# adaLN vectors turned by TensorE ahead of use, and two new written orders, in a hybrid encoder block

## The chip, the core and the metric

The kernel runs on one NeuronCore of a Trainium2 chip. The metric is the device time of one execution in microseconds (us). Five engines work side by side, each on its own list of instructions: TensorE (PE in the profile; its weight loads are PEld), VectorE (DVE), ScalarE (ACT), GpSimd (POOL, hardly used here) and SyncE (SP), whose list holds all DMA issues of this kernel.

## What is computed

One layer for 256 tokens of width 2048, in float32:

```
mod = silu(c) @ w_ada + b_ada                  # nine vectors of 2048: sh1 sc1 gt1 sh2 sc2 gt2 sh3 sc3 gt3
f = swiglu(modulate(rms_norm(h, g_ffn1), sh1, sc1), w1_gate, w1_up, w1_down)
h = h + 0.5 * gt1 * f
qkv = modulate(rms_norm(h, g_mix), sh2, sc2) @ w_qkv
o = concat(rms_norm(neighbourhood heads 0-7), rms_norm(dilated heads 8-15))
h = h + gt2 * (o @ w_o)
f = swiglu(modulate(rms_norm(h, g_ffn2), sh3, sc3), w2_gate, w2_up, w2_down)
h = h + 0.5 * gt3 * f
```

swiglu(x) = (silu(x @ w_gate) * (x @ w_up)) @ w_down with a hidden width of 5632; modulate(n, shift, scale) = n * (1 + scale) + shift.

## The kernel before, in words

**Products.** Every large product is made of three in a faster 32-bit format: an operand is split into a rounded high part (ScalarE, a cast) and the rest (VectorE, a subtraction), and high x high, high x low and low x high are summed. Weights come in chunks of 128 x 1024 (512 KB): `wraw` loads one into one of five "raw" buffers, `wsplit` casts it (`hiw`, L162) and subtracts (`low`, L165), which frees the raw buffer. The class `W` hands them out in order: `prepare(ahead)` splits chunks up to `ahead` (3) beyond the one in use, `chunk` returns the next. Split chunks have four buffers each.

**Stages.** (1) The first FFN's up-projection on hidden blocks 0 to 31, its down-projection, the up-projection on blocks 32 to 43 and their down-projection (`ffn_rest`, `ffn_down`). A down-projection goes through four pieces q = 0 to 3 of 512 output columns; piece by piece the residual `hq` is updated (`update`, L238 and L241), squared for the next norm (L254) and multiplied by the scale (`scaled`, L258). (2) q, k and v of four head groups, 96 units of one chunk each (`qkv_unit`), with the heads' attention (`head`: a transposes q and k, b makes scores and softmax, c transposes the weights, d multiplies v) spread over later units by the tables PLAN; then 32 units of `w_o` (`wo_unit`). LAST is unit 111, END unit 127. (3) The second FFN, as (1).

**The two boundaries.** From FFN to q, k, v, and from `w_o` to the second FFN, `cross` writes out the order of TensorE, VectorE and ScalarE by hand. The last four chunks of the old product (A) are done for the first half of the tokens, then for the second, so that norms of the first half can begin early. `Edge` does the norm: `most` and `rstd` the statistics, `normed(q, t)` the modulated norm of column quarter q for token half t (L281), `turned` four transposes on TensorE (L286), `split` the high and low parts of the result (L188, L189). Four chunks B of the next product follow for half 0 and then half 1 (`bpass`). `prep1` splits one chunk (cast and subtraction side by side in each engine's order), `extra` splits two of them into spare tiles, `keep_warm` issues matmuls on ones. Two of four quarters of half 1 are turned between the passes.

**The adaLN vectors.** `mod` is made of 144 dots on VectorE (L145), each over a 1 MB piece of `w_ada` loaded by SP (`ada_issue`, L135); vector j is complete after its 16 dots, as a tile `mods[j]` of 128 partitions x 16 columns. They run in the background: `bg_add` queues them, `bg_step` and `bg_use` issue a load or do a dot, at a rate per prepared chunk (`ws.pace`: RA, RB, RBD, RF) or at the units in COLUMNS; `bg_until(0)` does all that is queued. Vectors 0 and 1 go first, then 2, 4, 3, 5 and ten dots of 7 and 6, then the other 22 of 7 and 6 in the attention, and 8 in the second FFN. `begin`, which starts a boundary, sets the rate to zero, so dots left over then run in the attention, the last of them by `bg_until(0)` at unit LAST - 16.

Vectors 2 to 8 are needed as rows, the same 2048 numbers on every partition. `line_of(j)` writes the tile to DRAM as 16 x 128 numbers by one DMA whose access pattern swaps the two axes (L117), and `rows_of` reads the line back onto all partitions (L123).

**Who orders what.** Outside the written stretches a scheduler orders each engine's list from the program's order and a cost estimate. In the attention only TensorE's list is in program order (MANUAL); around both boundaries TensorE's, VectorE's and ScalarE's are (BORDER); SP's list is always the scheduler's. PSUM has eight banks, used as four pairs ("pair") in the up-projections and as eight single banks ("bank") elsewhere; `psum_pool` changes over.

Of the kernel before, what the change touches and what calls it, by code (L numbers as in the profile page):

```python
# [9 lines left out]
F32 = mybir.dt.float32  # L10
# [21 lines left out]
Q = 4  # L32
# [13 lines left out]
RF = 0.14  # L46
# [12 lines left out]
def build(tc, a):  # L59
    nc = tc.nc  # L60
    with ExitStack() as ctx:
# [105 lines left out]

        def wsplit_halves(raw, alloc):

            his, los = [], []  # L170
            for i in range(2):
                his.append(alloc("hih"))
                los.append(alloc("loh"))
                r = raw[:, i * QW : (i + 1) * QW]
                nc.scalar.copy(his[i], r)
                nc.vector.tensor_tensor(los[i], r, his[i].bitcast(F32), ALU.subtract)
            return his, los
# [65 lines left out]
        class Edge:  # L243
# [16 lines left out]
            def most(self, t):  # L260

                a, b = self.c[:, t, 0:1], self.c[:, t, 1:2]
                nc.vector.tensor_tensor(a, self.ss[:, t, 0:1], self.ss[:, t, 1:2], ALU.add)
                nc.vector.tensor_tensor(a, a, self.ss[:, t, 2:3], ALU.add)
# [23 lines left out]
            def split(self, q, t):  # L288
                b = self.bank[q, t].rearrange("p (k s) -> p k s", k=4)
                ts = slice(t * P, (t + 1) * P)  # L290
                split(b, nq[q][:, :, 0, ts], nq[q][:, :, 1, ts])

        def tok(ps, two, w, first, last, ts=(0, 1)):
# [19 lines left out]
            for t, l, r, st, sp_ in todo:  # L313
                nc.tensor.matmul(ps[t], l, r, start=st, stop=sp_)  # L314

        def cross(ps, twos, first, upd, edge, bpass, extra, after=None):
# [5 lines left out]
            edge.most(0)  # L322
            edge.most(1)
            ws.extra(2, extra)

            def rest(t):
                upd(t)
                edge.square(Q - 1, t, ps[t])
                edge.rstd(t)
# [4 lines left out]
            rest(0)  # L334
            edge.normed(0, 0)
            edge.normed(1, 0)
# [12 lines left out]
            ws.prep1()  # L349
# [842 lines left out]
```

## Time and profile before

| | us |
|---|---|
| median of 3 runs (lowest to highest) | 1957.53 (1956.42 to 1958.87) |
| the profiled execution | 1957.54 |
| its span, from the first to the last instruction | 1955.8 |
| PE busy | 1904.0 (97%) |
| DVE busy | 1483.8 (76%) |
| ACT busy | 889.0 (45%) |
| 16 DMA engines busy, queue q1 | 73.1% of their span |

A row of the waits tells who waited for whom, the sum in us, how often, and the longest. A row of the windows begins with the stretch in us from the span's start and its length, then for PE, PEld, DVE, ACT and POOL the busy time and number of instructions, then the granted TensorE clock (1.00 is full), the DMA engines' busy share and GB/s; a window of one line's instructions has that engine alone. A row of the timeline has start, length, engine, line, operation, out<-in, shape, number, and in brackets the idle time before it with what ended it. A row of the groups has the number of instructions, busy us, mean ns of one, and idle time before them. A DMA row has the number, KB each, and the median us from issue to landing. A row of the chain of waits has start, length and what it was.

### The profile page before, as it was taken

To read this page: it belongs to the slowest core of one execution; us is meant where nothing else is said; L and a number is where in the kernel's file an instruction comes from. 1 tells how busy PE (TensorE), PEld (TensorE's weight loads), DVE (VectorE), ACT (ScalarE), POOL (GpSimd) and SP (SyncE) were. 2 spreads that over 40 slices of the span, in tenths; PEclk is the share of its full clock that TensorE was granted. 3 is DMA by queue.
4 is the path that set the end of the run, shared out by engine and by line. 5 is a ranking of instruction groups with operands and counts; after the bars stand their busy time and mean duration, and the time that the engine had idled before them with its cause. 6 is when DMAs were issued, how large, how long until landed. Compare 5 with 4: busy or idle time off the path is not lost.

```text
span 1955.8 us, 25965 instructions
## 1 busy us (share of the span) xinstructions
PE 1904.0 (97%) x9868; PEld 1629.5 (83%) x9868; DVE 1483.8 (76%) x1940; ACT 889.0 (45%) x1293; POOL 0.7 (0%) x6
## 2 busy tenths in 40 slices
PE   9999999999999989899999798999999999999999
PEld 8888888888888878788878687788888888888887
DVE  6999999898788857888887886667676754555664
ACT  2544544434344434455555454545445443334542
POOL 0000000000000000000000000000000000000000
PEclk9999999999999999999999899999999999999999
DMA  9998888999889886688776773567767666555553
GB/s 399 403 355 321 324 310 314 300 367 401 308 345 345 316 213 207 224 332 296 249 254 208 211 260 128 170 234 244 237 244 246 229 201 209 194 186 191 193 196 139
DMA packets 138124, 513.38 MB, mean 262 GB/s; under 512 B 28176, under 2 KB 28688, under 8 KB 119568
## 3 DMA queue, kind: packets, MB, share of 16 engines
q1 hardware_dynamic: 138000, 511.74, 73.1%
q8 instruction: 77, 1.26, 0.3%
q14 instruction: 47, 0.39, 0.1%
HBM read 509.53 MB, written 2.15 MB: 262 GB/s over the span
## 4 chain that ended last, share of the span: by engine, by line
PE 66%; DVE 3%; DMA 2%; ACT 1%; issue 1%; SPq 0%; ACTq 0%
PE pb L543 20%; PE pd L314 17%; PE pb L537 10%; PE pqk L314 4%; PE pqv L314 4%; PE pqq L314 4%; PE po L314 3%; DMA rw<-in_w_e_dram 1%; DMA rw<-in_w_o_dram 1%; DVE low L165 1%; PE po L185 1%; PE pt L286 0%; ACT hiw L162 0%; SPq L135 0%; PE psc L185 0%
## 5 line engine op out<-in xcount | busy, mean ns | idle before, releaser
L165 DVE TENSOR_TENSOR low<-rw,hiw 128x1024 fp32r<-128x1024 f32 x640 | 774.3, 1221 | 334.1 <-ACT hiw L162 310.8
L162 ACT CAST hiw<-rw 128x1024 fp32r<-128x1024 f32 x640 | 669.6, 1052 | 671.5 <-PE pd L314 181.7
L543 PE MATMUL pb<-nq,hiw 128*128 128x512 f32 x2032 | 495.4, 390 | 1.1 <-DVE gu L588 0.7
L543 PEld LDWEIGHTS pb<-nq,hiw 128*128 128x128 f32 x2032 | 374.3, 188 | 74.3 <-DVE gu L588 1.0
L314 PE MATMUL pd<-hiw,hd 128*128 128x512 f32 x1408 | 352.7, 391 | 6.6 <-ACT hiw L162 5.7
L314 PEld LDWEIGHTS pd<-hiw,hd 128*128 128x128 f32 x1408 | 265.9, 189 | 62.8 <-ACT hiw L162 6.1
L537 PEld LDWEIGHTS pb<-nq,low 128*128 128x128 f32 x2032 | 262.1, 192 | 13.8 <-DVE low L165 5.3
L537 PE MATMUL pb<-nq,low 128*128 128x256 f32 x2032 | 269.9, 283 | 3.7 <-DVE low L165 3.7
L145 DVE CUSTOM_DVE_ANT_0 ra<-ra,cb,vec 128x2048 f32<-128x2048 f32 x111 | 260.2, 2344 | 7.5 <-DMA ra<-in_w_ada_dram 7.5
L314 PE MATMUL pd<-low,hd 128*128 128x512 f32 x704 | 190.7, 391 | 2.0 <-DVE low L165 2.0
L314 PEld LDWEIGHTS pd<-low,hd 128*128 128x128 f32 x704 | 132.5, 189 | 30.8 <-DVE low L165 3.2
L543 PE MATMUL pb<-nq3b,hiw 128*128 128x512 f32 x336 | 90.0, 390 | 0.0
L145 DVE CUSTOM_DVE_ANT_0 rx<-rx,cb,vec 128x2048 f32<-128x2048 f32 x33 | 77.4, 2345 | 3.0 <-DMA rx<-in_w_ada_dram 2.9
L543 PEld LDWEIGHTS pb<-nq3b,hiw 128*128 128x128 f32 x336 | 63.1, 188 | 13.6
L543 PE MATMUL pa<-nq,hiw 128*128 128x512 f32 x288 | 72.3, 393 | 0.0
L314 PE MATMUL po<-hiw,ox 128*128 128x512 f32 x256 | 68.5, 405 | 1.0 <-ACT hiw L162 1.0
L314 PE MATMUL pqk<-hiw,nq 128*128 128x512 f32 x256 | 65.0, 396 | 0.0
L314 PE MATMUL pqq<-hiw,nq 128*128 128x512 f32 x256 | 64.6, 394 | 0.0
L314 PE MATMUL pqv<-hiw,nq 128*128 128x512 f32 x240 | 62.0, 397 | 0.0
L543 PEld LDWEIGHTS pa<-nq,hiw 128*128 128x128 f32 x288 | 51.9, 189 | 9.3
L314 PEld LDWEIGHTS po<-hiw,ox 128*128 128x128 f32 x256 | 48.1, 193 | 12.0 <-ACT hiw L162 1.4
L587 ACT COPY gu<-pb 128x512 f32<-128x512 f32 x54 | 31.8, 588 | 54.7 <-PE pb L543 30.1
(192 smaller groups left out, 1592.0 us busy)
## 6 DMA issues: line engine op xcount, KB each, us to landing
ra<-in_w_ada_dram SPq DMA_DIRECT2D x111, 1024.0 KB, 7.0
rw<-in_w_b_dram SPq DMA_DIRECT2D x200, 512.0 KB, 4.6
rw<-in_w_d_dram SPq DMA_DIRECT2D x128, 512.0 KB, 5.2
rw<-in_w_c_dram SPq DMA_DIRECT2D x96, 512.0 KB, 4.3
rw<-in_w_qkv_dram SPq DMA_DIRECT2D x96, 512.0 KB, 4.9
rx<-in_w_ada_dram SPq DMA_DIRECT2D x33, 1024.0 KB, 7.5
rw<-in_w_e_dram SPq DMA_DIRECT2D x48, 512.0 KB, 4.6
rw<-in_w_a_dram SPq DMA_DIRECT2D x44, 512.0 KB, 6.2
```

Source lines behind the costliest of these rows:

```text
L145: dot = nc.vector.tensor_tensor_reduce(out=raw, in0=raw, in1=cb, scale=1.0, scalar=vec[:, BA + i : BA + i + 1], op0=ALU.mult, op1=ALU.add, ...
L162: cast = nc.scalar.copy(hi, raw)
L165: nc.vector.tensor_tensor(lo, raw, hi.bitcast(F32), ALU.subtract)
L185: nc.tensor.matmul(out, l, r, start=first and i == 0, stop=last and i == 2, **kw)
L314: nc.tensor.matmul(ps[t], l, r, start=st, stop=sp_)
L537: nc.tensor.matmul(out[:, :S], weights(b, 1), r[:, 0, :], start=False, stop=stop, skip_group_check=self.shared)
L543: nc.tensor.matmul(out, weights(b, 0), r, start=first, stop=last and b in early, skip_group_check=self.shared)
L587: nc.scalar.copy(u, p[..., :S])
```

## The change

- `line_of` transposes `mods[j]` on TensorE into a PSUM tile of 16 x 128, copies it to SBUF on VectorE (into a buffer with the tag "nt"), and writes it to DRAM in runs of 128 numbers.
- Lines 4 and 3 are made right after the first down-projection (before: in `begin`, after the second up-projection), line 5 at unit 66 (before 88), lines 7 and 6 at unit LAST - 8 (before LAST - 4), line 8 three hidden blocks before the end of the second FFN's first up-projection (before: after it). RF goes from 0.14 to 0.16.
- In the first FFN's second down-projection, `bg_until(0)` stands at piece q = 1.
- `prep1` and `extra` become `cast` and `sub`, placed apart from each other in `cross`; `split` of an edge becomes `hi` and `lo`. `cross` has a new order; half 1 of quarter 0 is turned inside the last pass of half 0; both halves of quarter 3 are turned in `end`; `keep_warm` is gone.
- Units 4 and 5 after the first boundary prepare one chunk ahead; so do chunks k = 8 to 11 after the second, which are handled one at a time (`group` 1, before 2).
- At the second boundary quarter 2 is scaled in `normed`; the last of the A chunks is prepared ahead of the updates; `bpass2` does the low weights of chunks 2 and 3 once for all 256 tokens instead of twice for 128.
- Heads 0 to 7 are scaled into float32 tiles that lie in the places of heads 12 to 15, and split into high and low at units 78, 80, ... 92.

```diff
-RF = 0.14
+RF = 0.16
...
         def line_of(j):
             lines[j] = dram.tile([KT, P], F32, tag=f"line{j}", name=f"line{j}")
-            nc.sync.dma_start(lines[j].rearrange("k p -> p k"), mods[j])
+            ps = pools["p"].tile([KT, P], F32, tag="b", name="lt")
+            nc.tensor.transpose(ps, mods[j], ident)
+            t = sp.tile([KT, P], F32, tag="nt", name="lt")
+            nc.vector.tensor_copy(t, ps)
+            nc.sync.dma_start(lines[j], t)
...
-            for t, l, r, st, sp_ in todo:
+            for i, (t, l, r, st, sp_) in enumerate(todo):
+                if i == 4 and mid:
+                    mid()
                 nc.tensor.matmul(ps[t], l, r, start=st, stop=sp_)
...
+            e = edge
...
+            ws.cast(extra)
+            ws.cast(extra)
+            ws.sub()
+            e.most()
+            upd(0)
+            e.square(Q - 1, 0, ps[0])
+            ws.sub()
+            e.rstd(0)
+            e.normed(0, 0)
+            e.normed(1, 0)
+            second(0)
+            ws.cast()
+            ws.sub()
             second(1)
             second(2)
-            edge.turned(0, 0)
+            e.turned(0, 0)
             second(3)
-            edge.turned(1, 0)
-            edge.split(0, 0)
-            edge.split(1, 0)
-            rest(1)
+            e.turned(1, 0)
+            e.hi(0, 0)
+            ws.cast()
+            e.lo(0, 0)
+            upd(1)
             if after:
                 after()
-            ws.prep1()
-            edge.normed(0, 1)
+            e.hi(1, 0)
+            e.square(Q - 1, 1, ps[1])
+            ws.sub()
+            e.lo(1, 0)
+            e.rstd(1)
+            e.normed(0, 1)
+            e.normed(1, 1)
+            ws.cast()
             B = [ws.take() for j in range(4)]
-            for j in range(3):
-                bpass(j, B[j], 0)
-            edge.turned(0, 1)
-            edge.split(0, 1)
-            bpass(3, B[3], 0)
-            keep_warm(2)
-            edge.normed(1, 1)
+            for j in range(4):
+                bpass(j, B[j], 0, (lambda: e.turned(0, 1)) if j == 3 else None)
+            e.hi(0, 1)
+            e.lo(0, 1)
+            e.normed(2, 0)
             bpass(0, B[0], 1)
...
+            e.turned(1, 1)
+            e.hi(1, 1)
+            ws.cast()
+            e.lo(1, 1)
+            e.normed(2, 1)
+            ws.sub()
             bpass(1, B[1], 1)
...
+            e.turned(2, 0)
+            e.turned(2, 1)
             bpass(2, B[2], 1)
...
             bpass(3, B[3], 1)
...
+            e.hi(2, 0)
+            e.hi(2, 1)
+            e.lo(2, 0)
+            e.lo(2, 1)
+            e.normed(3, 0)
+            e.normed(3, 1)
+            ws.sub()
 
             def end():
-                edge.turned(3, 1)
-                edge.split(3, 1)
+                for t in range(2):
+                    e.turned(3, t)
+                for t in range(2):
+                    e.hi(3, t)
+                    e.lo(3, t)
...
+                if edge is not None and q == 1:
+                    bg_until(0)
...
             ffn_down(range(F1), hid, row)
+            if begin:
+                line_of(4)
+                line_of(3)
...
-            units[u](ws.chunk())
+            units[u](ws.chunk(1 if u < 6 else None))
...
-                            edge[0].scaled(q, t)
+                            if q < 2:
+                                edge[0].scaled(q, t)
...
+                if b == 0:
+                    for hd in range(8):
+                        at(78 + 2 * hd, lambda hd=hd: split(raw_o[hd], ox[hd][:, 0, :], ox[hd][:, 1, :]))
...
+                    if hd < 8:
+                        nc.scalar.activation(raw_o[hd], po, AF.Copy, scale=go)
...
-                    if u == 88:
+                    if u == 66:
                         line_of(5)
...
-                    if u == LAST - 4:
+                    if u == LAST - 8:
                         line_of(7)
                         line_of(6)
+                    if u == END - ST:
+                        ws.prepare()
...
                 for half in range(2):
+                    if half and mid:
+                        mid()
+                    if half and j > 1:
+                        if t == 0:
+                            return
+                        ts = slice(0, S)
...
+            ws.group, ws.turn = 1, False
             for k in range(8, KT):
                 for f in range(NG):
                     for j in range(2):
+                        ws.ahead = 1 if k < 12 else AHEAD
                         ws.add(ps2[f][j], nx[k], False, k == KT - 1, key=(f, j))
...
         for f in range(NG, F1):
+            if f == F1 - 3:
+                ws.pace(0.0)
+                bg_until(0)
+                line_of(8)
             ps = pair("pb")
...
-        ws.pace(0.0)
-        bg_until(0)
-        line_of(8)
         ffn_rest(hid, 8, out=a["out"])
```

More of the change, by code (lines that the diff above doesn't have):

```diff
@@ L166, in wsplit @@
             return hi, lo
[L168 to L177, printed above, removed]
         def part_of(w, c, n):
@@ L286, in turned, with halves, hi, lo @@
                     nc.tensor.transpose(self.bank[q, t][:, j * P : (j + 1) * P], self.n[q, t][:, j * P : (j + 1) * P], ident)
-            def split(self, q, t):
+            def halves(self, q, t):
                 b = self.bank[q, t].rearrange("p (k s) -> p k s", k=4)
-                ts = slice(t * P, (t + 1) * P)
-                split(b, nq[q][:, :, 0, ts], nq[q][:, :, 1, ts])
-        def tok(ps, two, w, first, last, ts=(0, 1)):
+                return (b, *(nq[q][:, :, i, t * P : (t + 1) * P] for i in range(2)))
+            def hi(self, q, t):
+                b, hi, lo = self.halves(q, t)
+                nc.scalar.copy(hi, b)
+            def lo(self, q, t):
+                b, hi, lo = self.halves(q, t)
+                nc.vector.tensor_tensor(lo, b, hi.bitcast(F32), ALU.subtract)
+        def tok(ps, two, w, first, last, ts=(0, 1), mid=None):
             def whi(i):
@@ L358, in cross @@
-            edge.normed(1, 1)
-            bpass(0, B[0], 1)
-            edge.turned(1, 1)
-            edge.split(1, 1)
-            edge.normed(2, 0)
-            ws.prep1()
+            e.hi(1, 0)
[6 more added lines that the diff above has]
+            ws.cast()
+            B = [ws.take() for j in range(4)]
+            for j in range(4):
+                bpass(j, B[j], 0, (lambda: e.turned(0, 1)) if j == 3 else None)
@@ L466, in __init__ @@
                 self.thens = []
+                self.casts = []
                 self.ready = {}
@@ L474, in __init__, with cast, sub @@
                 self.ended_lo = False
-            def extra(self, n, alloc):
-                for i in range(n):
-                    assert self.head == self.tail + i
-                    self.ready[self.head] = wsplit_halves(wraw(srcs[self.head]), alloc)
-                    self.head += 1
-            def prep1(self):
-                self.ready[self.head] = wsplit(wraw(srcs[self.head]))
+            def cast(self, alloc=None):
+                raw = wraw(srcs[self.head])
+                if alloc:
+                    tiles = [(alloc("hih"), alloc("loh"), raw[:, i * QW : (i + 1) * QW]) for i in range(2)]
+                    self.ready[self.head] = [t[0] for t in tiles], [t[1] for t in tiles]
+                else:
+                    hi = wp.tile([P, CW], F32R, tag="whi", bufs=LOB, name="hiw")
+                    lo = wp.tile([P, CW], F32R, tag="wlo", bufs=LOB, name="low")
+                    tiles = [(hi, lo, raw)]
+                    self.ready[self.head] = hi, lo
+                for hi, lo, r in tiles:
+                    nc.scalar.copy(hi, r)
+                self.casts.append(tiles)
                 self.head += 1
+            def sub(self):
+                for hi, lo, r in self.casts.pop(0):
+                    nc.vector.tensor_tensor(lo, r, hi.bitcast(F32), ALU.subtract)
             def take(self):
@@ L791, in build @@
                     units.append(qkv_unit(len(units), g, j, nm, cch, st_))
-        end = ffn_rest(hid, 2, begin, order=order, bpass=lambda j, w, t: units[j](w, (t,)),
+        end = ffn_rest(hid, 2, begin, order=order, bpass=lambda j, w, t, mid=None: units[j](w, (t,), mid),
                        extra=lambda nm: hp.tile([P, QW], F32R, tag="hid", name=nm))
         for u in range(4, 8):
-            units[u](ws.chunk())
+            units[u](ws.chunk(1 if u < 6 else None))
             if u == 4:
@@ L816, in na_bias @@
                 return t
[L818 removed]
+            ox = [ac.tile([P, 2, S], F32R, tag=f"ox{i}", name=f"ox{i}") for i in range(12)]
+            raw_o = [ac.tile([P, 2, S], F32, tag=f"ox{i}", name=f"ro{i}") for i in range(12, NH)]
+            raw_o = [raw_o[i // 2][:, i % 2, :] for i in range(8)]
             ost = [Stat(), Stat()]
```

48 lines of the change are left out of this document (13 added, 35 removed).

## The prediction

> **What bounds the kernel now.** I read the core's span, then who ended TensorE's waits, then busy time in windows around each long wait. The span is 1955.8 us; the profiled execution took 1957.54 us, 1.74 us more, and that is also the median of the runs shown (1957.53 us). So the sum below is made against 1957.54.
>
> ```profile
> core 0: 1955.8 us, clock 0.992
> ```
> ```profile
> PE pT L896 <- DVE qn L854: 13.6, 3, 8.2
> PE pt L286 <- DVE gs L281: 13.0, 8, 2.9
> PE pd L314 <- ACT hiw L162: 5.7, 1, 5.7
> PE pb L537 <- DVE low L165: 3.7, 3, 2.1
> PE pP L937 <- DVE sc L931: 3.0, 2, 1.7
> ```
>
> The columns are: who waited, for whom, us in total, times, longest. TensorE sets the time, and there is little besides its own work to win: these five causes hold 39.0 us of waiting, 2% of the span. The question is therefore how much of 39 us the edit removes, and what it puts there. The same waits by place (us of the window, then PE busy; the clock stands after the five engines):
>
> ```profile
> 350.00:412.00 62.00, 59.15 (x301) 49.88 (x301) 55.96 (x78) 25.03 (x34) 0.00 (x0) 0.97 0.90 297
> 700.00:720.00 20.00, 14.31 (x62) 11.68 (x61) 4.73 (x6) 3.57 (x5) 0.00 (x0) 0.85 0.80 155
> 769.00:808.00 39.00, 33.71 (x157) 26.66 (x157) 27.77 (x48) 15.52 (x26) 0.00 (x0) 0.96 0.41 144
> 915.00:1030.00 115.00, 109.06 (x528) 90.50 (x527) 96.49 (x184) 60.76 (x135) 0.00 (x0) 1.00 0.72 254
> 1095.00:1121.00 26.00, 15.32 (x62) 11.88 (x61) 19.06 (x38) 6.03 (x7) 0.00 (x0) 0.80 0.80 231
> 1186.00:1243.40 57.40, 47.32 (x291) 40.81 (x289) 38.07 (x60) 23.11 (x39) 0.00 (x0) 0.97 0.38 128
> ```
>
> Window less PE busy gives idle: 2.85, 5.69, 5.29, 5.94, 10.68 and 10.08 us. After five of the waits the granted clock is 0.50 for a while:
>
> ```profile
> 389.90:393.20 3.30, 3.30 (x13) 2.91 (x13) 3.30 (x5) 2.01 (x3) 0.00 (x0) 0.50 0.87 323
> 714.20:720.90 6.70, 5.26 (x12) 4.13 (x13) 3.93 (x6) 3.45 (x6) 0.00 (x0) 0.50 1.02 403
> 785.90:789.20 3.30, 2.90 (x9) 2.51 (x10) 1.47 (x3) 0.59 (x1) 0.00 (x0) 0.50 0.43 159
> 1106.70:1116.80 10.10, 4.05 (x10) 3.08 (x11) 8.80 (x21) 2.68 (x3) 0.00 (x0) 0.50 0.74 160
> 1229.60:1232.90 3.30, 3.30 (x11) 2.62 (x10) 1.92 (x2) 1.53 (x2) 0.00 (x0) 0.50 0.02 6
> ```
>
> Work at half clock takes twice as long, so half of PE busy is lost there: 1.65, 2.63, 1.45, 2.03, 1.65 us. Idle and half clock together, by place: **350** 4.50, **700** 8.32, **769** 6.74, **915** 5.94, **1095** 12.71, **1186** 11.73. These are the prizes.
>
> **The written lines (350, 700, part of 1095).** Each adaLN vector goes to DRAM as one DMA that swaps partitions and columns, so every element is its own run:
>
> ```profile
> ra<-in_w_ada_dram SPq DMA_DIRECT2D x111, 1024.0 KB, 7.0
> ...
> out_dram<-hq SPq DMA_DIRECT2D x2, 128.0 KB, 1.9
> ...
> line<-m SPq DMA_DIRECT2D x7, 8.0 KB, 15.6
> ```
>
> 8 KB take 15.6 us, while 128 KB written in long rows take 1.9. Lines 4 and 3 are issued at the end of the first layer's second up-projection, and behind them a weight load hangs in the chain of waits:
>
> ```profile
> 695.58 18.87 DMA rw<-in_w_e_dram
> ...
> 1885.75 65.29 PE pd L314 x288
> ```
>
> The second row gives the price of a 512-wide matmul: 65.29 / 288 = 0.227 us, so a twelve-matmul down or qkv chunk is 2.72 us. With runs of 512 B the line write should land like the 1.9 us row, and it is written a whole up-projection earlier. I take all 8.3 at 700 (at worst 5.0, if the row loads, which stay, delay these chunks instead), and 3.0 of 4.5 at 350 (0 to 4.5): there line 2 is still written next to the down-projection's first loads, and VectorE is busy 55.96 of 62 us, a second reason for that wait.
>
> **The dots moved.** `bg_until(0)` now stands in the second down-projection, pieces 1 on. The code queues 32 + 64 + 10 = 106 dots ahead of the attention's own 22. By the rows below (x counts each dot and its accumulator read) 98 are done by 700 us, so eight move there, five with their loads, as three buffers can be full before. Six ran at 1075 until now:
>
> ```profile
> 0.00:700.00 700.00, 230.46 (x196) 1.00 0.89 340
> ...
> 1075.00:1112.00 37.00, 14.12 (x12) 0.93 0.80 268
> ```
> ```profile
> L165 DVE TENSOR_TENSOR low<-rw,hiw 128x1024 fp32r<-128x1024 f32 x640 | 774.3, 1221 | 334.1 <-ACT hiw L162 310.8 <-issue 15.1 <-PE pg L537 3.3
> ...
> L145 DVE CUSTOM_DVE_ANT_0 ra<-ra,cb,vec 128x2048 f32<-128x2048 f32 x111 | 260.2, 2344 | 7.5 <-DMA ra<-in_w_ada_dram 7.5
> ```
>
> Each dot holds VectorE 2.34 us. In 1095 to 1121 TensorE waits for the last group's normed q (`qn`, 13.6 us with one earlier wait), which sits in VectorE's queue behind such dots, and they wait for loads that share the DMA engines with lines 7 and 6. With no dot and no slow line there, a wait like those of 915's window should be left: three share 5.94 us, each behind one dot; I leave 1.5. Gain 11.2 (8 to 12.7). At the new place the eight dots need 8 x 2.34 = 18.7 us of VectorE. Room:
>
> ```profile
> 725.00:769.00 44.00, 44.00 (x196) 36.44 (x195) 32.72 (x39) 22.88 (x33) 0.00 (x0) 1.00 0.74 239
> ```
>
> 11.3 us idle there and, once the weight wait is gone, 15.3 in 700:720, some of it filled by the lows that the wait held back. It just fits, with three chunks of prepared weights as slack; cost 1.0 (0 to 7, all the overflow of 18.7 over 11.3).
>
> **First boundary (769).** Second half's norm waits behind a weight split:
>
> ```profile
> 784.36 1.23 DVE L165 TENSOR_TENSOR low<-rw,hiw 128x1024 fp32r<-128x1024 f32 x1 [0.52 <-ACT hiw L162]
> 785.50 0.74 DVE L281 SCALAR_TENSOR_TENSOR gs<-gs,e1c,row 128x512 f32<-128x512 f32 x1
> ```
> ```profile
> 786.30 1.11 PE L286 MATMUL pt<-ident,gs 128*128 128x128 f32 x4 [2.79 <-DVE gs L281]
> ...
> 803.53 0.70 PE L314 MATMUL pqv<-hiw,nq 128*128 128x512 f32 x2
> ```
>
> I put the new VectorE order on this clock, with 1.22 us for a weight's low, 0.74 for a norm and somewhat less for the other 128x512 operations. Until the turn of (1,0) nothing changes, since the norms of half 0 still wait for the update and its square. From there:
>
> VectorE now does the third weight's low, the lows of (0,0) and (1,0), the update of half 1, then waits for ScalarE's square of it, does the fourth weight's low (1.23 us, with 0.52 idle ahead) and only then the norm of (0,1). In the new order the update comes before the low of (1,0), 1.3 us earlier, and this low and the fourth weight's fill the time of the square. So the norm of (0,1) starts at 785.50 - 1.23 - 0.52, with the earlier update about 783.4, and ends at 784.1. TensorE asks for it four matmuls (0.9 us) later than now, at 784.2: no wait in place of 2.79. Then 0.3 us are lost until half 1 of quarter 0 is copied out. The norm of (2,0) runs in VectorE's idle time before the (1,1) low; that of (2,1) ends at 789.3, 0.4 us after TensorE has reached its turn. Both norms of quarter 3 are ready at 794.8, ahead of unit 4's end at 795.3, and both its turns follow. Unit 5, at 803.53 now, would start at 796.1, 7.4 us earlier (0.5 of it the dropped warm-up matmuls). The shorter lead of weights at units 4 and 5 costs nothing as long as a low stays under a chunk's 2.72; loads go out as raw buffers come free, not with the cast. The schedule leaves no room for hand-overs between engines, so I take 6.0 (2.9 to 7.4).
>
> **Second boundary (1186).** The same order, with three more edits: the last chunk is prepared ahead of the updates; the third quarter's scaling leaves VectorE's queue there; and two pairs of narrow groups become one wide group each:
>
> ```profile
> 1205.62 1.20 PE L1042 MATMUL pg<-nq,hih 128*128 128x256 f32 x8
> 1206.65 1.00 PE L1042 MATMUL pg<-nq,loh 128*128 128x128 f32 x8
> ```
>
> Of the narrow groups four at 1.00 become two at 1.20: 1.6 us. By the same hand schedule 0.5 us of waiting is left at the first turn, 1.4 where (0,1) must be copied out with no other matmul to put in front, 0.6 at (2,1), 0.8 before the next stage's first product as now, and 0.4 elsewhere: 3.7. The chunks of k = 8 to 11 no longer stand behind the last turn. From 11.7 + 1.6 - 3.7, and some pipeline fill at each wait saved, I get 10.5 (4.8 to 13.3, the upper end with no wait left).
>
> **The cost of turning.** Seven transposes join TensorE's work, seven copies VectorE's. Eight narrow matmuls in a row take 1.00 us (0.13 each), four transposes after a wait 1.11 (0.28 each): 0.9 to 2.0 us. I take 1.0, by the row without a wait, for the vectors are complete by then. Dearer may be the PSUM buffer. Lines 2, 4 and 3 stand right where the pools change, so the next stage's first accumulator may have to wait for VectorE's copy, queued behind updates. Four operations of 128x512, 0.74 us each as in row 785.50, at two places make 5.9 us; if the scheduler gives another buffer, it is nothing. I take 1.5, nearer to nothing: the stages change over without such a wait in the five causes above. Lines 5 (unit 66) and 7, 6 (unit 103) have fixed places in TensorE's order, long after their last dots; SP issues three small writes there, landing like the 1.9 us row under the units that follow, and line 5's rows are loaded 29 units later as now. Line 8 is turned three column blocks before its stage ends instead of in the next: counted as nothing. Each copy holds one of two "nt" buffers until its write has landed; the tanh that shares them comes once in four chunks, 10.9 us.
>
> **Heads split later (915).** Eight splits leave VectorE's queue in the stretch with the waits for `sc` (3.0 us in two) and come back at units 78 to 92, two units apart; each is 128x256, so half of the 0.74 us of twice the size. ScalarE, 60.76 of 115 us busy, gets eight more casts. The parked outputs take the places of heads 12 to 15, needed 16 units after the last split: no wait. VectorE's order there is the scheduler's, and the dots stay in the columns: gain 1.0 (-3 to 3).
>
> **Sum.** 3.0 + 8.3 + 11.2 + 6.0 + 10.5 + 1.0 = 40.0 gained; 1.0 + 1.5 + 1.0 = 3.5 paid; 36.5 net: 1957.54 - 36.5 = **1921 us**.
>
> **Half clock.** Rows 389.9 and 785.9 show it after waits of no more than 2.1 and 2.8 us, so by these rows one or two of the waits that I leave may cost 1.6 us each on top, and the time would be 1924. [...]
>
> **Rivals.** (1) The boundaries' waits move rather than go: VectorE's chain, 27.77 of 39 us busy, stays what ends last. For it: every wait there names VectorE. Against: the written order puts weight lows behind norms. Then they give 2.9 and 4.8, 8.8 us less: 1930. (2) Loads, not lines, starve the stages: five ada loads beside the w_e chunks, and row loads which still follow their line on SP. Then 8.3, 3.0 and half of 11.2 stay lost, 16.9: 1938. Against: 8 KB at 15.6 us. (3) Slower: the scheduler queues the moved loads and dots in series. Place: second down-projection, piece 1. A load takes 7.0 us and its dot 2.34; five in series and three more dots make 53.7 us, less a lead of three chunks (8.2): 45.5 us of wait, and 1957.5 - 36.5 + 45.5 = 1966. It decides once four of the five loads run so; up to then the gains pay for it. For: lows wait behind dots in VectorE's queue. Against: dots at 1075 to 1112 ran six in 37 us. (4) The lines stay in step with the old waits because turns are scheduled as late as the DMAs were, and the boundary gains are eaten by new bank waits: about 1957.
>
> **How the numbers follow.** Chances: forecast 0.58, (1) 0.20, (2) 0.12, (3) 0.06, (4) 0.04. A change of 0.2%, 3.9 us, is about what a measurement can tell. Faster is forecast, (1) and (2): 0.90; same 0.04; slower 0.06. The lower end takes the upper bounds of all gains (4.5 + 8.3 + 12.7 + 7.4 + 13.3 + 3 = 49.2) at no cost: 1908. The upper end reaches past (2) to 1940. (3), (4) and the tails of (2) are left out, under 2 in 10.
>
> **What would show it.** Line writes landing in 2 to 4 us; no wait of TensorE over 2 us near 710, 1100 or 1230; no dots between 806 and 812 or after unit 85; first wide chunk after the second boundary some 35 us earlier. Wrong would be: half clock near the second down-projection, pd or pb waiting for the copy of a turned line, or a boundary as long as now.

## The result, and the profile after

The changed kernel takes 1925.80 us (median of 6 runs, 1922.57 to 1927.67); the kernel before, run beside it, 1956.98 (1955.99 to 1960.31). The ratio is 0.9835, with a 95% interval of 0.9822 to 0.9847: 31 us faster. The forecast was 1921 in 1908 to 1940. The profiled executions are 35.0 us apart (1957.54 and 1922.57), where 36.5 was forecast; what follows compares these two. The profiled execution of the changed kernel is the fastest of its six, so the medians are only 31.2 us apart.

Span and clock of the changed kernel, and TensorE's longest waits by cause (waiting tile, releaser, us in total, times, longest):

```profile
core 0: 1920.8 us, clock 0.997
```
```profile
PE pd L316 <- DVE lt L120: 7.2, 1, 7.2
PE pt L279 <- DVE gs L274: 2.7, 3, 1.8
PE pd L316 <- DVE low L169: 2.7, 2, 1.6
PE pd L316 <- ACT hiw L166: 2.3, 2, 1.9
PE pT L927 <- DVE qn L881: 2.2, 1, 2.2
```

The two causes that led the list before, `qn` with 13.6 us and `gs` with 13.0, are down to 2.2 and 2.7. On top stands a wait that was not there: `lt` is the turned line in PSUM. The same places by window (us of the window, PE busy, weight loads, VectorE, ScalarE, GpSimd, granted clock, DMA share, GB/s):

```profile
350.00:412.00 62.00, 54.83 (x285) 47.16 (x284) 58.58 (x82) 25.20 (x34) 0.00 (x0) 0.92 0.84 301
390.20:400.40 10.20, 5.01 (x12) 3.97 (x13) 10.20 (x16) 2.27 (x4) 0.00 (x0) 0.50 0.83 286
700.00:745.00 45.00, 41.13 (x194) 33.64 (x193) 38.28 (x44) 19.54 (x25) 0.00 (x0) 1.00 0.88 336
769.00:808.00 39.00, 38.40 (x183) 31.19 (x183) 31.44 (x50) 19.76 (x33) 0.00 (x0) 1.00 0.57 192
905.00:1020.00 115.00, 112.66 (x549) 93.75 (x548) 98.61 (x188) 64.65 (x146) 0.00 (x0) 1.00 0.75 261
1075.00:1101.00 26.00, 26.00 (x123) 21.28 (x123) 19.74 (x42) 13.78 (x34) 0.00 (x0) 1.00 0.65 215
1170.00:1227.40 57.40, 53.59 (x346) 47.88 (x346) 44.55 (x69) 30.72 (x50) 0.00 (x0) 1.00 0.44 153
```

Around 1095 TensorE is busy in every one of 26 us (15.32 of 26 before), in the first boundary 38.40 of 39 (33.71). Only the first row is worse than its twin: idle went from 2.85 to 7.17 us, and one stretch at half clock is left, of 10.2 us, where there were five. The written lines land in 2.7 us by the median, as forecast, but single ones took 1.4 to 8.7 us (lines 4 and 3 the longest):

```profile
line<-lt SPq DMA_DIRECT2D x7, 8.0 KB, 2.7
```

To compare stretches that have moved, I call the **excess** of a stretch the sum, over its matmuls, of the time from one start to the next less the median of that time for matmuls of the same line and shape. It holds idle time and half clock alike.

| stretch of the work | excess before | after | gained | on record |
|---|---|---|---|---|
| 350 to 412, first down-projection begins | 5.9 | 9.9 | -4.1 | 3.0, less part of 1.5 |
| 412 to 700 | 3.1 | 3.2 | -0.1 | 0 |
| 700 to 745, second down-projection begins | 8.5 | 4.8 | 3.7 | 8.3 less 1.0 |
| 745 to 812, first boundary | 7.9 | 1.4 | 6.5 | 6.0 |
| 812 to 1030, attention | 7.8 | 4.1 | 3.6 | 1.0 |
| 1030 to 1121 | 14.0 | 1.7 | 12.3 | 11.2 |
| 1121 to 1250 (1240 after), second boundary | 15.8 | 6.1 | 9.7 | 8.9 |
| second layer's down-projection begins | 1.3 | 0.0 | 1.3 | 0 |
| fewer and wider matmuls, less the turns | | | 2.3 | 1.6, less 1.0 |

The terms add up to 35.2; the rest, -0.2, lies spread over the other stretches. A second execution of the same program (e5 below) has an excess of 8.8, 6.1 and 5.8 us in the first, third and fifth row, so these rows are good to some 1.7 us; the last section shows why.

### The profile page after: what moved, and what is told of

The parts are those of the page before. It is cut to its first block, busy times and chain, and to the rows that moved or that the text cites. A ratio compares the mean times of both kernels' runs of the same rounds, so it can differ in the third digit from the quotient of the medians.

```text
span 1920.8 us, 25930 instructions
## 1 busy us (share of the span) xinstructions
PE 1893.1 (99%) x9851; PEld 1623.1 (84%) x9851; DVE 1484.4 (77%) x1939; ACT 891.5 (46%) x1301; POOL 0.7 (0%) x6
## 4 chain that ended last, share of the span: by engine, by line
PE 69%; DVE 2%; DMA 1%; ACT 0%; issue 0%; SPq 0%; ACTq 0%; DVEq 0%
PE pb L565 20%; PE pd L316 16%; PE pb L559 11%; PE pqk L316 5%; PE pqq L316 5%; PE pqv L316 4%; PE po L316 4%; PE pg L1086 1%; PE psc L178 1%; PE po L178 1%; DMA ra<-in_w_ada_dram 0%; DMA row<-line 0%; PE pg L565 0%; PE pP L968 0%; PE pt L279 0%; PE pT L927 0%
## 5 line engine op out<-in xcount | busy, mean ns | idle before, releaser
L169 DVE TENSOR_TENSOR low<-rw,hiw 128x1024 fp32r<-128x1024 f32 x632 | 764.7, 1221 | 307.4 <-ACT hiw L166 291.8
L166 ACT CAST hiw<-rw 128x1024 fp32r<-128x1024 f32 x632 | 661.3, 1052 | 652.0 <-PE pd L316 205.6
L149 DVE CUSTOM_DVE_ANT_0 ra<-ra,cb,vec 128x2048 f32<-128x2048 f32 x109 | 255.6, 2345 | 6.9 <-DMA ra<-in_w_ada_dram 6.8
L149 DVE CUSTOM_DVE_ANT_0 rx<-rx,cb,vec 128x2048 f32<-128x2048 f32 x35 | 82.1, 2345 | 3.3 <-DMA rx<-in_w_ada_dram 3.3
L565 PEld LDWEIGHTS pb<-nq3b,hiw 128*128 128x128 f32 x336 | 63.1, 188 | 13.6
```

What stands on the lines that cost most here:

```text
L149: dot = nc.vector.tensor_tensor_reduce(out=raw, in0=raw, in1=cb, scale=1.0, scalar=vec[:, BA + i : BA + i + 1], op0=ALU.mult, op1=ALU.add, ...
L166: cast = nc.scalar.copy(hi, raw)
L169: nc.vector.tensor_tensor(lo, raw, hi.bitcast(F32), ALU.subtract)
L565: nc.tensor.matmul(out, weights(b, 0), r, start=first, stop=last and b in early, skip_group_check=self.shared)
```

## The experiments

Eleven kernels ran, each in several rounds beside the kernel before, whose median was 1957.7, 1958.6 and 1958.1 us in the three sets. Ratios are to it. The program of the changed kernel was measured twice, as itself and as e5: 0.9835 and 0.9824, 2 us apart, and smaller differences of medians are not read. In the texts on record, A and B are the two explanations that a run was to tell apart.

### Line 2's turn: which PSUM buffer it takes

The new wait, in the timeline of the changed kernel (start, us, engine, line, operation):

```profile
387.95 0.27 PE L118 MATMUL lt<-ident,m 128*16 128x128 f32 x1
388.95 0.42 DVE L614 SCALAR_TENSOR_TENSOR pt<-th,pt 128x256 f32<-128x256 f32 x1
389.29 2.35 DVE L149 CUSTOM_DVE_ANT_0 ra<-ra,cb,vec 128x2048 f32<-128x2048 f32 x1
...
393.50 1.22 DVE L169 TENSOR_TENSOR low<-rw,hiw 128x1024 fp32r<-128x1024 f32 x1
394.63 0.42 DVE L614 SCALAR_TENSOR_TENSOR pt<-th,pt 128x256 f32<-128x256 f32 x1
394.97 0.27 DVE L120 COPY lt<-lt 16x128 f32<-16x128 f32 x1
395.39 3.75 PE L316 MATMUL pd<-hiw,hd 128*128 128x512 f32 x8 [7.17 <-DVE lt L120]
```

In the kernel before the line's DMA left at 354, soon after the last of its dots; a turn has a place in TensorE's order, and that is 388. Its copy stands in VectorE's queue behind a dot, a weight's low and the folds of two column blocks, 6 us of work without a gap, and `pd` waits for the copy. Does it wait because of the turn, or because VectorE is full?

**e1_line2_early**: 1923.38 us, ratio 0.9827 (0.9815 to 0.984).

```diff
             for f in range(NF1, F1):
+                if f == F1 - 4:
+                    line_of(2)
                 ps = pair("pb")
...
         hid = ffn(K1, part, rest1)
-        line_of(2)
```

> Edit: the changed kernel with line 2's turn moved from behind the first layer's first up-projection to four column blocks before its end (its last dot is done at 337.7 us, the turn stands at 387.9 in the changed kernel). Theory A, the turned line's PSUM buffer: the 7.2 us wait of the first down-projection product is the wait for a 0.27 us copy that stands behind a queue of VectorE work, and the half clock behind it follows from it. Then both go: the excess over the matmuls' own pitch between 350 and 412 us, 9.9 us in the changed kernel, falls to 1 to 3 us, no half clock stands there, and the time is 7 to 9 us under the changed kernel's median of 1925.8: 1917 to 1919. Rival B, VectorE is simply full there: the first products wait for the weights' lows or the hidden state in the place of the copy, the excess stays at 6 or more, and the time is 1922 to 1926.

The wait for the copy went, and another took its place (waits by cause):

```profile
PE pd L319 <- DVE pt L608: 5.8, 1, 5.8
```

Excess 8.9: B by its numbers. But the releaser is telling: it is the fold of the very last accumulator of the up-projection (the fold adds an accumulator to the hidden tile on VectorE, and frees its bank). The built programs, not the traces, list the bank of every PSUM tile. The pairs come in the order 0, 6, 4, 2 (first bank of each), and the first `pd` of the new pool always takes bank 0:

```
                  last accumulators, in order      first pd (bank 0) follows
before            0, 6, 4, 2                       the fourth-last accumulator
changed kernel    0, 6, 4, 2, line 2 in 0          the line
e1                line 2 in 0; 6, 4, 2, 0          the last accumulator
e9 (below)        0, 6, 4, 2, warm in 0, line in 6 the warm-up matmul, which nobody reads
```

So the line's place in the pool's rotation decides, not its place in time. **e5_skip_pair** (1924.53 us, 0.9824, 0.9811 to 0.9838) was meant to test that:

```diff
+        pair("skip")
         line_of(2)
```

> Edit: one line in the changed kernel: a PSUM pair is allocated and not used just before line 2 is turned, so that the turned line takes the second of the four pairs in place of the first. Theory A, the turn shifts the rotation: 56 accumulators went through four pairs before, so the first down-projection product, which always takes the first banks of the new pool, followed the fourth-last accumulator; with the line as 57th it follows the line itself, and with the line moved ahead it followed the very last accumulator (5.8 us). With the skipped pair it follows the fourth-last again: the wait of pd for the line's copy goes, the half clock shrinks to one step or none, the excess between 350 and 412 us goes from 9.9 to 2 to 4, and the time is 1917 to 1921. Rival B, VectorE's backlog: ten operations stand in its queue whichever bank is used, so pd waits for a low or a fold there instead, the excess stays at 7 or more, and the time is 1923 to 1927.

The edit was empty: a tile that nothing writes gets no bank, and the line stayed in 0. The wait was there (6.5 us); the run tells nothing of A or B, and serves as a second measurement of the changed kernel. **e9_warm_pair** gives the extra pair a matmul:

```diff
+        keep_warm(1)
         line_of(2)
```

> Edit: one 128-column warm-up matmul into a PSUM pair of its own just before line 2 is turned. An allocated pair that nothing writes was not placed at all by the pool (the run with the skipped pair had the program of the changed kernel, the line still in bank 0); this one is written, so the line lies in banks 6 and 7 and the first down-projection product follows the fourth-last accumulator in banks 0 and 1, as in the kernel before. Theory A, rotation: the wait of pd for the line's copy (6.5 to 7.2 us in every run so far) goes, the excess between 350 and 412 us falls from 8.8 to 9.9 to 2 to 5, the half clock there shrinks to one step of 3.4 us or none, and the time is 4 to 7 us under that of the changed kernel (1924 to 1926): 1918 to 1921. Rival B, VectorE's backlog: pd or the second down-projection product waits for a low or a fold in its place, the excess stays at 7 or more, 1923 to 1926.

1919.88 us, ratio 0.9815 (0.9801 to 0.9829). The timeline of this run:

```profile
388.25 0.27 PE L118 MATMUL lt<-ident,m 128*16 128x128 f32 x1
388.56 2.08 PE L316 MATMUL pd<-hiw,hd 128*128 128x512 f32 x8
...
395.44 0.27 DVE L120 COPY lt<-lt 16x128 f32<-16x128 f32 x1
```

The copy is as late as ever, and nobody waits for it. Excess 3.3 instead of 9.9, no half clock there. Theory A holds: one warm-up matmul (its first record starts at 388.03, the turn at 388.25, so 0.22 us) that moves a tile to another bank takes 6.6 us away from this stretch. Not all of it reaches the end: in this execution the excess is 1.2 us higher from 412 to 700 and 2.4 from 700 to 745, so that the profiled executions are 2.7 us apart; the ratios are 3.9 us apart, the medians 5.9.

### Writing turned or element by element

**e2_columns**: 1941.26 us, ratio 0.9917 (0.9904 to 0.9929), 15 us slower than the changed kernel. Nothing is turned; the places are the new ones.

```diff
-            ps = pools["p"].tile([KT, P], F32, tag="b", name="lt")
-            nc.tensor.transpose(ps, mods[j], ident)
-            t = sp.tile([KT, P], F32, tag="nt", name="lt")
-            nc.vector.tensor_copy(t, ps)
-            nc.sync.dma_start(lines[j], t)
+            nc.sync.dma_start(lines[j].rearrange("k p -> p k"), mods[j])
```

> Edit: the changed kernel with every line written as before (one DMA that swaps partitions and columns, no turn, no copy), at the new places. Theory A, place: what the second down-projection gained came from writing lines 4 and 3 130 us before their rows are loaded, so writes of 15 us harm nothing there; without the turns the 7.2 us wait at 388 goes back to the kernel before's waits at 350 to 412 (excess 5.9 in place of 9.9), 2 us of transposes go too, and lines 7 and 6 written beside the output projection's loads near 1101 cost 0 to 4 us. Time 1918 to 1924, no slower than the changed kernel. Rival B, speed: element-wise writes starve the loads beside them wherever they stand, so waits of over 3 us for weights come back near 570 and 1105, and the time is 1930 to 1938.

A fell: an early element-wise write still costs, where it stands. B's time is exceeded too. Rows from the timeline around 570 us (SPq is SyncE's DMA queue):

```profile
556.42 10.02 SPq L117 DMA_DIRECT2D line<-m  x2
566.54 9.42 SPq L156 DMA_DIRECT2D rw<-in_w_c_dram  x4
...
583.58 1.04 ACT L162 CAST hiw<-rw 128x1024 fp32r<-128x1024 f32 x1 [16.21 <-DMA rw<-in_w_c_dram]
584.68 1.65 PE L561 MATMUL pb<-nq,hiw 128*128 128x512 f32 x3 [5.96 <-ACT hiw L162]
```

Lines 4 and 3 hold SP for 10.0 us, where the turned ones took 0.88. The four loads queued behind them follow at 566.54, and the next one to be cast lands only at 583.48: 5.96 us of wait, then half clock (the three matmuls of the last row take 1.65 us; three in the kernel before take 0.84 at full clock, at 385.82), 10.2 us of excess between 560 and 600 where the changed kernel has 1.5. The DMA engines have a part in it besides SP: the two lines take 19.7 and 23.8 us to land (12.9 is the median of the seven), and meanwhile the engines are busy and move next to nothing (the last two figures of a window are their busy share and GB/s):

```profile
568.00:576.00 8.00, 6.82 (x35) 5.68 (x34) 6.28 (x8) 0.00 (x0) 0.00 (x0) 1.00 0.82 24
```

Lines 7 and 6, which no turn binds to TensorE's order here, go out at 1039 and 1052. The first of them holds SP for 0.43 us only, and yet the next two weight loads, issued at 1042.43 and 1046.10, take 11.9 and 9.6 us to land, where 3.4 is usual there in the changed kernel. So such a write delays loads even where it does not hold SP; how much of the delay at 570 is SP's was not separated. At 1072 a cast waits 6.8 us for its load, and the stretch near 1077 loses 5.9 us. And a wait at 1221 did not fit, of the first `pb` of the second layer's up-projection for the last `pg`:

```profile
PE pb L561 <- DVE gu L606: 5.5, 1, 5.5
```

**e6_columns_bank** (1943.37 us, 0.9917, 0.9903 to 0.9931) was to tell banks from loads:

```diff
+            nc.sync.dma_start(lines[j].rearrange("k p -> p k"), mods[j])
+            pools["p"].tile([KT, P], F32, tag="b", name="lt")
```

> Edit: the kernel with element-wise writes at the new places, and with each line still taking its PSUM buffer, unused, so that every later tile of the pools lies where it lies in the changed kernel. It separates two costs that came together in the run without turns (1941 us): loads that wait behind the slow writes (near 578 and 1077) and the wait of the first pb for the last pg at 1221 (5.5 us, 8.4 with its half clock), which theory A puts down to the rotation of buffers. A: the wait at 1221 goes, the ones at 578 and 1077 stay, 1932 to 1936. B: the wait at 1221 comes from late weights like the others and stays: 1939 to 1943. By A the writes themselves cost 7 to 10 us more than turned ones, by B 14 or more.

Empty as e5 was: the same banks, the same time. **e11_columns_turned** writes the tile:

```diff
+            nc.sync.dma_start(lines[j].rearrange("k p -> p k"), mods[j])
+            ps = pools["p"].tile([KT, P], F32, tag="b", name="lt")
+            nc.tensor.transpose(ps, mods[j], ident)
```

> Edit: every line is turned by TensorE into its PSUM buffer as in the changed kernel, but the result is not copied and not used: the line is written element by element from its columns. So the banks of all later tiles are those of the changed kernel (the accumulators of the second layer's first products in 2, 5, 7 and 6; in the element-wise kernel 2, 3, 6 and 0, and the next stage's first accumulator takes 0). It separates what the run with the unused buffer could not, since that buffer was not placed. Theory A, rotation: the wait of pb for the last pg at 1221 (5.0 to 5.5 us and half clock) goes, those for weights near 578 and 1077 stay, there is no wait for a line's copy at 388: 1932 to 1936. Rival B, late weights: the wait at 1221 stays and the time is 1940 to 1944.

1934.53 us, ratio 0.9881 (0.9867 to 0.9894). Its waits by cause:

```profile
PE pb L563 <- ACT hiw L164: 7.6, 2, 7.2
...
PE pP L966 <- DVE sc L960: 3.8, 1, 3.8
```

The weights' wait stays, the one for `pg` is gone (in e2 the last `pg` lay in bank 0, which the next pool's first tile takes; here in 6), and so is a 1.1 us wait where the second layer's down-projection begins. A: of e2's 15 us, 7 were rotation, and writing turned rather than by elements is worth 9 us at the new places, although the wait for line 2's copy, which e11 does not have, is still in the changed kernel.

### The dots

**e3_dots_back**: 1929.67 us, ratio 0.986 (0.9848 to 0.9873).

```diff
-                if edge is not None and q == 1:
-                    bg_until(0)
```

> Edit: the changed kernel without the flush of the queue of dots in the second down-projection, so that eight dots run in the attention again. Theory A, dots: the 12.7 us that the stretch around 1100 lost in the kernel before came from dots ahead of the last group's normed q in VectorE's queue and their loads; then 6 to 12 us come back there with waits of pT for qn, the 4.4 us of waits at 733 to 740 go, and the time is 1927 to 1934. Rival B, lines: the two element-wise writes and the row loads that waited for them held the stretch; now that lines are fast, the dots fit, the stretch loses under 3 us, and the time is 1920 to 1924.

```profile
PE pT L925 <- DVE qn L879: 11.5, 3, 6.8
```

The wait for the last group's `qn` is back, without any slow line (7 and 6 go out at 1109 here, after the waits): excess 13.5 between 1075 and 1125, as in the kernel before (13.6). A: the dots alone suffice for that loss. Between 700 and 740, on the other hand, nothing is lost now, so the flush costs 4.8 us there. The median moved by 3.9 us, the profiled execution by 6.3. In the changed kernel that stretch reads:

```profile
730.76 2.35 DVE L149 CUSTOM_DVE_ANT_0 ra<-ra,cb,vec 128x2048 f32<-128x2048 f32 x1
733.03 2.35 DVE L149 CUSTOM_DVE_ANT_0 rx<-rx,cb,vec 128x2048 f32<-128x2048 f32 x1
...
734.14 1.04 ACT L166 CAST hiw<-rw 128x1024 fp32r<-128x1024 f32 x1 [3.73 <-DMA rw<-in_w_e_dram]
...
735.24 2.11 PE L316 MATMUL pd<-hiw,hd 128*128 128x512 f32 x8 [1.87 <-ACT hiw L166]
735.38 2.35 DVE L149 CUSTOM_DVE_ANT_0 ra<-ra,cb,vec 128x2048 f32<-128x2048 f32 x1
737.65 1.22 DVE L169 TENSOR_TENSOR low<-rw,hiw 128x1024 fp32r<-128x1024 f32 x1
738.85 2.35 DVE L149 CUSTOM_DVE_ANT_0 ra<-ra,cb,vec 128x2048 f32<-128x2048 f32 x1
738.92 1.20 PE L316 MATMUL pd<-low,hd 128*128 128x512 f32 x4 [1.57 <-DVE low L169]
```

Three dots follow each other for 6.9 us with no weight's low between them, while a chunk's 2.72 us goes by twice. Only the second wait is a dot's in VectorE's queue: the low at 737.65 stands behind the dot of 735.38, though its cast was done at 735.18. The first is a late load's: the cast at 734.14 waited 3.73 us for it. Its raw buffer, and four more, had been freed by lows between 717 and 725, but the five loads into them went out at 727.69 and from 733.57 on. SP's list has loads of dots ahead of them, and these waited for earlier dots to free their buffers (SP's longest wait from 715 to 746, and rows of its list):

```profile
SPq L139 <- DVE m L149: 13.6, 2, 8.6
```
```profile
727.27 0.33 SPq L139 DMA_DIRECT2D ra<-in_w_ada_dram  x1
727.69 0.38 SPq L160 DMA_DIRECT2D rw<-in_w_e_dram  x1
733.14 0.33 SPq L139 DMA_DIRECT2D ra<-in_w_ada_dram  x1
```

In e3, which has no such loads there, each weight load from 717 us on leaves within 0.2 us of the low that frees its buffer. **e8_rates** spreads the dots over the stages ahead: 1918.22 us, ratio 0.9791 (0.9778 to 0.9804).

```diff
-RBD = 0.45
+RBD = 0.49
...
-            ws.pace(up_rate)
+            ws.pace(0.43 if begin else up_rate)
```

> Edit: the changed kernel with the rate of dots per weight chunk raised from 0.45 to 0.49 in the first down-projection and from 0.33 to 0.43 in the second up-projection, so that about seven of the eight dots that the second down-projection now holds run before 700 us. Theory A, crowding: four dots back to back at 730 to 741 make the 4.8 us of excess between 700 and 745; VectorE is idle for 19 us between 560 and 700 and 25 us between 412 and 560, so the dots fit there, 3.5 to 5 us are won: 1920 to 1923. Rival B, loads: the DMA engines are 0.84 to 0.98 busy in these stretches, so the extra loads hold back weights and 2 us or more of new waits come up between 412 and 700: 1924 to 1932.

```profile
560.00:700.00 140.00, 140.00 (x783) 122.64 (x782) 124.02 (x140) 62.36 (x81) 0.00 (x0) 1.00 0.91 350
700.00:745.00 45.00, 45.00 (x215) 37.88 (x214) 32.83 (x41) 23.54 (x31) 0.00 (x0) 1.00 0.83 299
```

TensorE is busy throughout 700 to 745, and the DMA engines, at 0.91 from 560 to 700, carry the extra loads at no cost. A. The size is less sure than the place: 7.6 us by the medians, 3.2 between the profiled executions, and e8's has one more step of half clock, near 1012: eight 512-wide matmuls from 1011.36 take 3.55 us, in the changed kernel 2.07 (from 1016.22).

### The written orders, and the heads

**e4_old_orders** (the kernel before, with all other parts of the change): 1942.03 us, ratio 0.9924 (0.9912 to 0.9936). Against the changed kernel, `cross`, `tok`, `Edge`, `cast` and `sub`, `bpass2` and the lines that call them go back:

```diff
-            ws.cast(extra)
-            ws.cast(extra)
-            ws.sub()
-            e.most()
-            upd(0)
...
+            edge.most(0)
+            edge.most(1)
+            ws.extra(2, extra)
...
```

> Edit: the kernel before with everything of the change except the written orders at both boundaries (turned lines at their new places, dots moved, heads split later). Theory A, the orders did it: excess 8.0 us returns at the first boundary and about 14 at the second, with four narrow groups in place of two wide ones; 6.5 + 9.7 + 2 = 18 us more than the changed kernel: 1941 to 1946. Rival B, the boundaries were held in part by what ran beside them (element-wise writes of lines, dots and row loads), which is gone here too: less than 12 us come back, 1930 to 1937.

```profile
PE pt L290 <- DVE gs L285: 13.1, 8, 2.9
```

The eight waits for `gs`, 13.0 us before, are back to a tenth. A: with every other part of the change in place, 16 us of it are the orders. They were put back as one; which of their edits gave how much was not tried.

**e7_heads_back**: 1928.05 us, ratio 0.9844 (0.9831 to 0.9857).

```diff
-                    if hd < 8:
-                        nc.scalar.activation(raw_o[hd], po, AF.Copy, scale=go)
-                    else:
...
+                    nc.scalar.activation(ox[hd][:, 0, :], po, AF.Copy, scale=go)
+                    nc.vector.scalar_tensor_tensor(
+                        ox[hd][:, 1, :], po, go, ox[hd][:, 0, :].bitcast(F32), ALU.mult, ALU.subtract)
```

> Edit: the changed kernel with the first eight heads split at once, as in the kernel before. Theory A, the later split is what took the waits near 923 and 1000 away: 2 to 4 us come back between 905 and 1030 us (excess 3.7 in the changed kernel, 7.3 in the kernel before), 1928 to 1930. Rival B, these waits went with the element-wise write of a line and with the order that the earlier boundary leaves behind: the excess between 905 and 1030 stays under 4.5 and the time is that of the changed kernel within 2 us, 1924 to 1927, or lower, since eight late splits are gone from the output projection.

```profile
PE pP L963 <- DVE sc L957: 3.0, 2, 1.7
```

The very cause of the kernel before, `sc` with 3.0 us in two waits, is back, and the excess from 905 to 1030 is 7.5 (7.5 before; 3.7 in the changed kernel, 5.4 in e5, e8 and e10, where one step of half clock falls there). A by the trace; the whole kernel's times are 2 us apart, with intervals that overlap.

### Both repairs together

**e10_both** has the warm-up matmul of e9 and the rates of e8: 1913.54 us (1912.40 to 1917.80), ratio 0.9778 (0.9765 to 0.9792).

```diff
-RBD = 0.45
+RBD = 0.49
...
-            ws.pace(up_rate)
+            ws.pace(0.43 if begin else up_rate)
...
+        keep_warm(1)
         line_of(2)
```

> Edit: the warm-up matmul ahead of line 2's turn and the raised rates of dots (0.49 and 0.43) together. If the two are independent (A), their gains add: 1918.2 of the rates less 4 to 7, 1911 to 1914, with no wait of TensorE over 2.3 us left but the qn one near 1010. If the faster dots fill VectorE's queue behind the pool change (B), the first down-projection waits for lows instead, and the time stays at 1916 to 1919.

```profile
core 0: 1910.8 us, clock 0.999
```
```profile
PE pd L316 <- DVE low L169: 3.5, 4, 1.2
PE pt L279 <- DVE gs L274: 2.7, 3, 1.8
PE pT L928 <- DVE qn L882: 2.2, 1, 2.2
```

The gains add: 7.6 and 5.9 us apart, 12.3 together by the medians (10.0 between the profiled executions), and the longest wait is 2.2 us.

## Why the prediction was right, and where not

The waits that the sum was mostly made of, those at the boundaries and near 1095, went as forecast (28.5 of 35 us). That the sum came within 1.5 us is in part luck. By the medians it is 5 us off; two of its terms were 7 and 4 us too good, and smaller ones made up for them: heads (2.6 better than forecast), matmuls and turns (1.7), boundaries (1.3), line 8 (1.3) and 1095 (1.1).

- **Line 2 (350): wrong.** The step that failed is "Four operations of 128x512 [...] at two places make 5.9 us; [...] I take 1.5, nearer to nothing". The mechanism was named, with `pd` waiting for the copy of a turned line as the sign of it; the price was not. The queue was taken to hold four updates. It held a dot of 2.35 us, a low of 1.22 and seven smaller operations, and the wait, 7.2 us, brought 10.2 us of half clock. Which buffer the turn takes was left open ("if the scheduler gives another buffer, it is nothing"); that the count of tiles taken before settles it, so that the very next stage follows the turn, was not worked out. e1 and e9 show it. The 3.0 us of gain became a loss of 4.1.
- **700: half right.** The wait for weights at 709 went whole, and with the dots put back (e3) nothing is lost in the stretch. In e2, with element-wise writes at the new places, the stretch loses 5.1 us, hardly more than in the changed kernel, so the earlier place alone takes that wait away; turned lines at the old place were not tried. The step that failed is "It just fits, with three chunks of prepared weights as slack; cost 1.0": total room of VectorE was set against total work, but the dots' loads wait in SP's list for dots before them, with weight loads behind. 4.8 us, inside the bounds of 0 to 7.
- **1095: right in size (11.2, measured 12.3), wrong in one cause.** The prediction gave a part to the slow lines 7 and 6; in e3 the dots bring the whole loss back without them. The kernel before shows it too: line 7 goes out at 1103.52, when the last dot's load (issued at 1099.16, landed in 6.9 us) is on its way. Slow lines without dots were not tried at that place.
- **Boundaries: right.** 6.0 and 10.5 on record, 6.5 and 9.7 + 1.6 measured, and rival (1) falls. Of the second boundary's leftovers, 3.7 us by the forecast, the trace has 4.8: 1.95 instead of 0.5 at the first turn, 1.56 (1.4) where (0,1) is copied out, 0.8 (0.6) at (2,1), and nothing before the next stage, whose first accumulator now follows a bank read early.
- **Turning: dear on paper only.** A turn's record lasts 0.27 us, but the next matmul starts 0.03 us after the turn's start in four cases and 0.11 in two (the seventh is line 2's): 0.3 us in all, not 1.0.
- **Heads: right mechanism, too small.** 1.0 on record, 3.6 measured, undone by e7 (3.8). Where the wait for `qn` that remains brings a step of half clock, as in e5, the gain is 2.0.
- **Line 8** was counted as nothing and gave 1.3 us, by rotation again: before, the down-projection's first tile followed the second-last accumulator, now the third-last.
- **Rivals.** (2), starving loads, fell at 700 (e3: no wait there); it holds for element-wise writes at other places (e2). Of (3) a part came: two loads waited in series for their dots, and 4.8 us were lost, not 45.5. The new bank wait of (4) came, at one place of two.
- **The signs.** First wide chunk after the second boundary at 1209.59 instead of 1243.36: 33.8 us earlier, 35 forecast. No dots run between 806 and 812 or from 1068 to 1240. Lines land in 2 to 4 us by the median only. And one sign of being wrong came true: `pd` waits for the copy of a turned line.

## What to carry to other kernels

A helper that takes a buffer out of a rotating pool moves every later tile of that pool: before a pool changes, look up which tile lay last in the bank that the next stage takes first, and put there the one that is read earliest. Room for background work is not a sum over a stage; it has to be there between two deadlines, so spread it at a rate rather than flush it. And a transfer costs more than its own time through what is queued behind it: in SP's list weight loads stood for up to 8.6 us behind a dot's load that waited for its buffer, and behind an element-wise write weight loads took 11.9 us to land in place of 3.4.

## What the runs showed of the hardware

Half clock followed waits of TensorE. The kernels' ends left out, a stretch of it, at a granted clock of 0.50, lasted 3.4, 6.8 or 10.2 us in the traces of the two kernels: before, 3.4 from 389.9, 785.8 and 1229.5, 6.8 from 714.1 and 10.2 from 1106.7; after, 10.2 from 390.2. A step is 3.4 us of it. The 512-wide matmuls of the changed kernel start 0.427 us apart there and 0.227 at full clock (medians), which is 1.88 times as long, where the forecast took twice. The length of a wait alone does not settle whether half clock follows: in the kernel before it came after a wait of 2.09 us that ended at 389.70, and not after those of 2.91 and 2.25 us that ended at 1026.03 and 1203.22 (the granted clock is 1.00 from 1022 to 1030 and from 1200 to 1210). What settles it was not shown. The same wait for `qn`, 2.18 us long, in e5 and in the changed kernel (timeline row of the wait, then the next 3.4 us with the clock after the five engines):

```profile
1017.13 0.33 PE L928 MATMUL pT<-ident,qn 128*128 128x128 f32 x1 [2.18 <-DVE qn L882]
```
```profile
1017.40:1020.80 3.40, 3.40 (x10) 2.63 (x9) 0.69 (x1) 0.59 (x1) 0.00 (x0) 0.50 0.88 311
```
```profile
1016.13 0.33 PE L927 MATMUL pT<-ident,qn 128*128 128x128 f32 x1 [2.18 <-DVE qn L881]
```
```profile
1016.50:1019.90 3.40, 3.40 (x18) 2.88 (x17) 1.18 (x2) 1.94 (x4) 0.00 (x0) 1.00 0.80 272
```

In e5 10 matmuls run in these 3.4 us, at 0.50, in the changed kernel 18, at 1.00. By the two times above one step costs up to 1.6 us; the excess from 905 to 1030 is 5.4 in e5 and 3.7 in the changed kernel. This is a part of the spread between runs of one kernel.
